# Diagonal 32x32 products and a small masked tile in the chunkwise recurrence

## The chip, the cores and the metric

The kernel runs on one core of one Trainium2 chip, in one launch. The metric is the device time of that core in microseconds (us). The engines are TensorE (PE, with its weight loads shown apart as PEld), VectorE (DVE), ScalarE (ACT), GpSimd (POOL) and SyncE (SP, which issues DMAs).

## The reference

The network has two layers over 1024 tokens of 1024 channels. The first mixes tokens with a gated linear recurrence (HGRN2), the second with a causal convolution; each is followed by a squared-ReLU MLP with 4096 hidden channels. The change touches the recurrence of the first layer alone:

```python
def chunkwise_gated_recurrence(q, k, v, b):      # chunks of C = 32, 8 heads, dk = dv = 128
    def step(S, inp):
        qc, kc, vc, bc = inp                     # bc: cumulative sum of log f inside the chunk
        diff = bc[..., :, None, :] - bc[..., None, :, :]
        decay = jnp.where(causal, jnp.exp(jnp.where(causal, diff, 0.0)), 0.0)
        scores = jnp.einsum('bhtd,bhsd,bhtsd->bhts', qc, kc, decay)
        o = (jnp.einsum('bhts,bhsv->bhtv', scores, vc)
             + jnp.einsum('bhtd,bhdv->bhtv', qc * jnp.exp(bc), S))
        b_last = bc[..., -1:, :]
        S = (jnp.exp(b_last)[..., 0, :, None] * S
             + jnp.einsum('bhsd,bhsv->bhdv', kc * jnp.exp(b_last - bc), vc))
        return S, o
    ...
```

`q` is the silu of one projection, `f` the forget gate, `k = 1 - f`. The weight of a pair (s, t), s not after t, is the product of q at t, k at s, and all gates between them, summed over the 128 channels.

## The kernel before

**The stage.** All engines' orders are written out by hand (`manual_schedule`). One stage of the program makes the projections q, forget and output gate of all eight heads from x, in products of 128x512 on PE (`pair_product`, line 815; tiles `xf` and `fs`, in 12 matmuls to a product). A product is four slots of three matmuls; after each slot, `slot` (line 842) advances a tick counter and, at a set pace, the recurrences that are under way (`recs`, `active`, `step`, line 827). So the matmuls of a recurrence stand between those of the projections in PE's queue. At most two heads are under way, and the second starts when the first has done LAG = 9 steps. A job given to `later(n, job)` (line 353) is recorded n ticks on; that is how work for DVE and ACT is set behind the matmuls that it reads. Beside the recurrence, DVE and ACT split the weights of the projections into two parts (`make_form`, lines 543 to 574: a cast on ACT at line 571 and a subtraction on DVE, tile `fs`) and take the products out of PSUM (`evacuate`, line 768: the copy `t<-ps` on ACT at line 781 or an addition on DVE). Three PSUM banks serve the projection's products; a product's copy on ACT has to be done before a later product accumulates in the same bank, which is the next but one or later.

**One head's recurrence** (`recurrence(h)`, line 591) works on all 1024 tokens of the head at once, in chunks of P = 128 tokens, 8 chunks to a head (`2 * NTB`). Q and K hold channels on partitions and tokens along the free axis. The weights of a chunk, tile `A` (name `at`: partition s, chunk, t), are built level by level. At each level n the gates of half a block are multiplied into Q or K (`scale(n)`), and products of K and Q then give the weights of pairs whose distance that level covers:

- `levels(K, Q)` after scales 1, 2 and 4 gives pairs in one block of 16 but in different blocks of 8; `levels(kd[:, 1], kd[:, 0])` gives pairs in one block of 8; a second `levels(K, Q)`, after `scale(8)`, gives pairs in one block of 32 but in different blocks of 16. Each call is 8 matmuls of 128x128, one to a chunk, into `level_ps` (PSUM banks 3 and 4), all columns of it.
- After each, `put(i)` copies the wanted entries into `A` by `copy_predicated` with the i-th mask, on DVE, over 8 chunks x 128 columns = 1024 elements of each partition.
- Two loops (n = 32, 64; lines 653 to 659) add the pairs farther apart: 16 matmuls of 32x32 after `scale(16)` and 8 of 64x64 after `scale(32)`, written into `level_ps` at their place right of the diagonal, at partitions 0 and 64 for n = 32 and 0 for n = 64. The third mask takes in everything right of the blocks of 16, so `put(2)`, after `scale(64)`, lays these out as well.

PE is fed step by step; `scale(8)` and `put(1)` are recorded a tick after the first `levels`, `put(0)` a tick after the second, `scale(16)` a tick after the third, and `put(2)` a tick after the loop of 64. Since all three `levels` calls write the same part of `level_ps`, the second waits for `put(1)` and the third for `put(0)`.

Then K is transposed (`kt`, copied out by ACT at line 668), the state is carried from chunk to chunk (`outer`, `chain` on DVE, tile `state`), and `attend` multiplies `A` and the state with values and queries. ACT squares and scales the result (lines 679 and 685), it is transposed, and stored.

`A` is set to zero once, by POOL (line 940). The masks are three tiles of 128x128, loaded once by SP (line 939). Both lie in a room of tiles laid out from line 929.

Of the kernel before, what the change touches and what calls it, by code (L numbers as in the profile page):

```python
# [10 lines left out]
I32 = mybir.dt.int32  # L11
# [4 lines left out]
P = 128  # L16
# [5 lines left out]
NTB = HT // P  # L22
# [215 lines left out]
def body(ctx, tc, d, out):  # L238
    nc = tc.nc
# [53 lines left out]
    vector = Clocked(nc.vector, bg.dve, vector_cost)  # L293
    tensor = Clocked(nc.tensor, bg.pe, tensor_cost)
# [49 lines left out]
    wide_t, rows = (HT,), (NTB, P)  # L344
# [8 lines left out]
    def later(n, job):  # L353
        if n:
            waiting.append((ticks[0] + n, job))
        else:
            job()
# [99 lines left out]
    for k in range(4):  # L457
        c = slice((k % 2) * HT, (k % 2 + 1) * HT)
# [117 lines left out]
    level_ps, out_ps = (banks[:, k : k + 2].rearrange("p k (a b) -> p (k a) b", b=P) for k in (3, 5))  # L576
# [3 lines left out]
    def mul(o, a, b):  # L580
        vector.tensor_tensor(out=o, in0=a, in1=b, op=ALU.mult)

    def cutout(t, at, dims):
        return bass.AP(tensor=t.tensor, offset=t.offset + at, ap=[t.ap[0], *dims])

    def load_values(i, at=None):
        h, half = divmod(i, 2)
        vts[i] = vs() if at is None else at
        nc.sync.dma_start(out=vts[i], in_=vd[h // 4][half][:, :, h % 4 * P : (h % 4 + 1) * P])

    def recurrence(h):
        B = qk[h]
        Q, K = B[:, 0], B[:, 1]
        n2 = 2 * HT
        F, T = p1("f"), p1("T")
        totals = {1: F}
        at = 0
# [4 lines left out]
        def total(n):  # L602
            t = totals[n].rearrange("p (b s) -> p s b", s=2)
            mul(totals[2 * n], t[:, 0], t[:, 1])

        def scale(n):
            nb = n2 // (2 * n)
            o = cutout(Q, n, [[n2 - n, 2], [2 * n, nb], [1, n]])
            mul(o, o, cutout(totals[n], 0, [[1, 2], [2, nb], [0, n]]))

        def levels(a, b):
            for s in range(0, n2, P):
                tensor.matmul(level_ps[:, s // P, :], a[:, s : s + P], b[:, s : s + P], start=True, stop=True)

        def put(i):
            vector.copy_predicated(A, mask[:, i : i + 1, :].to_broadcast([P, 2 * NTB, P]).bitcast(I32), level_ps)

        vector.tensor_scalar(out=F, in0=K, scalar1=GATE_EPS, scalar2=None, op0=ALU.max)
        mul(Q, Q, F)
# [8 lines left out]
        rt, kd = p1("rt"), p1("kd")  # L628
# [7 lines left out]
        yield  # L636
        total(8)
        yield
        levels(K, Q)
        total(16)  # L640
        later(1, lambda: (scale(8), put(1)))
        yield
        levels(kd[:, 1], kd[:, 0])
        total(32)
        later(1, lambda: put(0))
        yield
        if h == H - 1:
            load_values(2 * h, F[:, :HT].rearrange("p (a b) -> p a b", a=NTB))
        levels(K, Q)
        total(64)  # L650
        later(1, lambda: scale(16))
        yield
        for n in (32, 64):
            for s in range(0, n2, 2 * n):
                c, r = divmod(s, P)
                tensor.matmul(level_ps[r : r + n, c, r + n : r + 2 * n], K[:, s : s + n], Q[:, s + n : s + 2 * n], start=True, stop=True)
            if n == 32:
                later(1, lambda: scale(32))
                yield
        dec = p1("dec")  # L660
        later(1, lambda: (scale(64), put(2), vector.tensor_copy(out=dec, in_=totals[P])))
        yield
        yield
        nk = 2 * NTB - 1
# [46 lines left out]
        def values(c):  # L711
            return vts[2 * h + c // NTB][:, c % NTB]
# [14 lines left out]
        def attend(cs):  # L727
            for c in cs:
                tensor.matmul(out_ps[:, c, :], A[:, c, :], values(c), start=True, stop=c == 0)
                if c:  # L730
# [96 lines left out]
    def step():  # L827
        if recs and (not active or len(active) == 1 and active[0][2] >= LAG):
            active.append([recs[0], recurrence(recs.pop(0)), 0])
        if not active:  # L830
            return False
        if not (len(active) == 1 and active[0][0] == H - 1 and active[0][2] >= LAG):
            alone[0] = not alone[0]
            if alone[0]:
                return True
        for one in list(active):
            one[2] += 1
            if next(one[1], one) is one:
                active.remove(one)
        return True  # L840
# [82 lines left out]
    for _ in range(5):  # L923
# [5 lines left out]
    p1 = Room(  # L929
        ((144, 152), (164, 172), (136, 144), (172, KBYTES)),  # L930
        {
            "qk": ((2, 2 * HT), 3), "kd": ((2, 2 * HT), 1), "at": (chunks, 1), "f": (two_t, 1), "T": (two_t, 1), "kt": (chunks, 1), "t": (wide_t, 4),
            "sq": (wide_t, 2), "u": (wide_t, 2), "mask": ((3, P), 1), "rt": ((2 * P,), 1), "state": ((P,), 8), "dec": ((2 * NTB,), 2),
        },
    )
    vs = ring((124, 126), rows, "v")
    mask = p1("mask")
    A = p1("at")
    nc.sync.dma_start(out=mask, in_=d["mask"])
    nc.gpsimd.memset(A, 0.0)  # L940
    for i in range(2):
        load_values(i)

# [52 lines left out]
    def gain(kb, name, layer):  # L996
        return vec(kb, f"{name}_g", layer), vec(kb + 4, f"{name}_b", layer)
# [75 lines left out]
    g, b = gain(192, "ln_mix", 0)  # L1073
# [257 lines left out]
    g, b = gain(184, "ln_ffn", 0)  # L1331
# [237 lines left out]
    g, b = gain(120, "ln_ffn", 1)  # L1569
# [22 lines left out]
def _layout(inputs):  # L1592
    import numpy as np

    i = {k: np.asarray(v) for k, v in inputs.items()}
    c = np.ascontiguousarray
    x = i["x"][0]
    r = {"x": c(x), "xT": c(x.reshape(2, HT, KB, P).transpose(0, 3, 2, 1))}
    w = i["a_w_in"][0]

    def cols(m, n):
        return m.reshape(KB, P, n, P).transpose(2, 1, 0, 3)

    def wide(m):
        return m.reshape(4, 2, P, 2, HT).transpose(3, 0, 2, 1, 4)

    q, f, g = [cols(w[:, k * D : (k + 1) * D], H).reshape(H, P, 2, HT).transpose(0, 2, 1, 3) for k in (0, 1, 3)]
    r["wp"] = c(np.stack([np.concatenate([q[j], f[j]] if kind == "q" else [g[2 * j], g[2 * j + 1]]) for kind, j in PAIRS]))
    r["wv"] = c(wide(w[:, 2 * D : 3 * D])).reshape(4, 2, P, 1024)
    r["wout"] = c(wide(i["a_w_out"][0])).reshape(2, 4, P, 1024)  # L1610
    r["wpw2"] = c(wide(i["b_w_pw2"][0])).reshape(2, 4, P, 1024)
    p = i["b_w_pw1"][0]
    r["wpw1"] = c(np.stack([cols(p[:, :D], KB), cols(p[:, D:], KB)], 1)).reshape(KB, 2, P, 1024)
    r["w1"] = c(cols(i["ffn_w1"][1], 32)).reshape(32, P, 1024)

    w1 = i["ffn_w1"][:1].reshape(1, 2, 4, P, NFC, 2, 2, P)
    r["w1q"] = c(w1.transpose(0, 4, 6, 1, 3, 5, 2, 7)).reshape(1, NFC, 4, P, 1024)
    w2 = i["ffn_w2"].reshape(2, NFC, 2, 2, P, 2, HT)
    r["w2"] = c(w2.transpose(0, 1, 5, 3, 4, 2, 6)).reshape(2, NFC, 4, P, 1024)

    def chan(v):
        return v.reshape(-1, P).T

    r["par"] = c(
        np.concatenate(
            [chan(i[n][0]) for n in ("a_norm_g", "a_lb_logits", "b_b_pw1", "b_b_dw", "b_ln_g", "b_ln_b")]
            + [i["b_w_dw"][0].reshape(TAPS, KB, P).transpose(2, 1, 0).reshape(P, KB * TAPS)],
            1,
        )
    )  # L1630
    s, t = np.arange(P)[:, None], np.arange(P)[None, :]
    m = np.zeros((P, 3, P), np.float32)
    m[:, 0] = (s // 8 == t // 8) & (s <= t)
    m[:, 1] = (s // 16 == t // 16) & (s // 8 < t // 8)
    m[:, 2] = s // 16 < t // 16
    r["mask"] = m
    for n in ("ln_mix_g", "ln_mix_b", "ln_ffn_g", "ln_ffn_b"):
        r[n] = c(i[n])
    r["b_pw2"] = c(i["b_b_pw2"])
    return r  # L1640
# [16 lines left out]
```

## Time and profile before

| What | us |
|---|---|
| median of 3 runs | 2118.72 (2116.82 to 2122.96) |
| the profiled execution's own time | 2120.82 |
| its span, first to last instruction | 2119.0 |
| stage of projections and recurrence, from the span's start | 88 to 450 |

Busy times in the span: PE 2086.5, PEld 1731.7, DVE 1447.1, ACT 1037.4, POOL 390.0. Busy time counts a moment once, however many instructions overlap in it. PE's fp32 matmuls of the recurrence each leave two records in the trace, so 8 matmuls show as x16. A row of the timeline gives the start, the time until the last of its instructions ended, and how many there are; since matmuls overlap, what a row costs PE is read from its start to the next row's start. In brackets stands how long the engine had been idle and what ended that. A row by form gives busy time, mean duration of one in ns, and idle time ahead of the group with its releasers.

### The profile page before, as it was taken

To read this page: it belongs to the slowest core of one execution; us is meant where nothing else is said; L and a number is where in the kernel's file an instruction comes from. 1 tells how busy PE (TensorE), PEld (TensorE's weight loads), DVE (VectorE), ACT (ScalarE), POOL (GpSimd) and SP (SyncE) were. 2 spreads that over 40 slices of the span, in tenths; PEclk is the share of its full clock that TensorE was granted. 3 is DMA by queue.
4 is the path that set the end of the run, shared out by engine and by line. 5 is a ranking of instruction groups with operands and counts; after the bars stand their busy time and mean duration, and the time that the engine had idled before them with its cause. 6 is when DMAs were issued, how large, how long until landed. Compare 5 with 4: busy or idle time off the path is not lost.

```text
span 2119.0 us, 27037 instructions
## 1 busy us (share of the span) xinstructions
PE 2086.5 (98%) x10056; PEld 1731.7 (82%) x10056; DVE 1447.1 (68%) x1868; ACT 1037.4 (49%) x1593; POOL 390.0 (18%) x384
## 2 busy tenths in 40 slices
PE   8999999999999999999999999999999999999998
PEld 7888787888888888888888888888878888888887
DVE  8697788877775665665666997899436443654456
ACT  5445454541465555544444677378443443433333
POOL 0112212201000000000002897299001000000001
PEclk9999999999999999999999999999999999999999
DMA  4778889771589786989997654564694987855542
GB/s 182 235 176 212 234 226 243 191 257 70 170 256 316 261 280 226 365 327 336 350 335 285 265 193 184 210 256 150 190 334 159 353 308 288 327 204 190 196 161 100
DMA packets 173494, 508.62 MB, mean 240 GB/s; under 512 B 16433, under 2 KB 45361, under 8 KB 172337
## 3 DMA queue, kind: packets, MB, share of 16 engines
q1 hardware_dynamic: 157872, 448.16, 59.0%
q0 software_dynamic: 15488, 58.72, 12.1%
q8 instruction: 79, 1.29, 0.2%
q14 instruction: 55, 0.44, 0.1%
HBM read 377.32 MB, written 196.61 MB: 271 GB/s over the span
## 4 chain that ended last, share of the span: by engine, by line
PE 78%; DVE 9%; DMA 6%; POOL 3%; issue 2%; ACT 2%; SPq 0%; DVEq 0%; POOLq 0%; ACTq 0%
PE ps L173 78%; POOL cb L173 3%; DVE qk L173 2%; DMA wa<-ready 1%; DMA raw<-in_w_dram 1%; DVE t L173 1%; DMA y<-kept 1%; DVE fs L173 1%; DMA vr<-in_wv_dram 1%; DMA hf<-ht 1%; DMA raw<-in_w1q_dram 1%; DVE xf L173 1%; DVE at L173 0%; DMA dh<-hf 0%; DVE vr L173 0%
## 5 line engine op out<-in xcount | busy, mean ns | idle before, releaser
L173 PE MATMUL ps<-dw,dh 128*128 128x512 f32 x2688 | 611.3, 389 | 0.0
L173 PEld LDWEIGHTS ps<-dw,dh 128*128 128x128 f32 x2688 | 504.1, 188 | 104.9 <-ACT dh L70 0.5
L173 PE MATMUL ps<-x1f,fw 128*128 128x512 f32 x1344 | 308.5, 390 | 1.1 <-DVE c L173 0.9
L173 PEld LDWEIGHTS ps<-x1f,fw 128*128 128x128 f32 x1344 | 251.2, 188 | 54.0 <-issue 1.3
L173 PE MATMUL ps<-xa,wa 128*128 128x512 f32 x1152 | 268.8, 392 | 0.0
L173 PE MATMUL ps<-xf,fs 128*128 128x512 f32 x1008 | 251.1, 400 | 1.7 <-ACT t L781 0.8
L173 PEld LDWEIGHTS ps<-xa,wa 128*128 128x128 f32 x1152 | 214.2, 188 | 43.5
L173 POOL TENSOR_TENSOR cb<-cb,prod 128x512 f32<-128x512 f32 x176 | 234.6, 1342 | 17.5 <-ACT prod L1425 7.0
L173 PEld LDWEIGHTS ps<-xf,fs 128*128 128x128 f32 x1008 | 185.6, 190 | 40.2 <-DVE t L173 2.2
L173 DVE TENSOR_TENSOR dh<-dh 128x1024 fp32r<-128x1024 f32 x112 | 136.4, 1222 | 114.5 <-ACT dh L70 113.8
L173 DVE TENSOR_TENSOR dw<-dr,dw 128x1024 fp32r<-128x1024 f32 x112 | 136.6, 1222 | 105.6 <-ACT dw L70 105.0
L173 DVE SCALAR_TENSOR_TENSOR ps<-u,par,ps 128x512 f32<-128x512 f32 x288 | 198.6, 748 | 9.9 <-ACT ps L1437 8.5
L70 ACT CAST dh<-dh 128x1024 fp32r<-128x1024 f32 x112 | 117.0, 1050 | 146.5 <-DMA dh<-hf 146.0
L70 ACT CAST dw<-dr 128x1024 fp32r<-128x1024 f32 x112 | 117.4, 1053 | 135.9 <-PE ps L173 124.5
L173 PE MATMUL ps<-xc,wa 128*128 128x512 f32 x768 | 174.4, 389 | 0.0
L474 POOL TENSOR_TENSOR mv<-mv,nhalf 128x1 f32<-128x1 f32 x32 | 45.2, 1414 | 686.3 <-DVE mv L173 686.3
L173 PEld LDWEIGHTS ps<-xc,wa 128*128 128x128 f32 x768 | 144.1, 188 | 29.9
L1425 ACT ACTIVATE prod<-u,par 128x512 f32<-128x512 f32 x176 | 125.4, 722 | 54.3 <-POOL cb L173 53.7
L173 DVE TENSOR_TENSOR wa<-raw,wa 128x1024 fp32r<-128x1024 f32 x51 | 66.5, 1306 | 67.9 <-ACT wa L70 67.8
L70 ACT CAST wa<-raw 128x1024 fp32r<-128x1024 f32 x51 | 53.6, 1050 | 117.5 <-PE ps L173 109.6
L1288 POOL COPY next<-ss 128x1 f32<-128x1 f32 x37 | 17.3, 467 | 410.9 <-DVE spare L173 259.6
L173 PE MATMUL ps<-w,oT 128*128 128x512 f32 x384 | 89.2, 391 | 0.8 <-ACT oT L872 0.8
(198 smaller groups left out, 2685.4 us busy)
## 6 DMA issues: line engine op xcount, KB each, us to landing
wa<-ready SPq DMA_DIRECT2D x122, 512.0 KB, 4.2
dh<-hf SPq DMA_DIRECT2D x112, 512.0 KB, 5.2
sum_w<-in_w_dram POOLq DMA_DIRECT2D x40, 1024.0 KB, 10.8
ready<-spare SPq DMA_DIRECT2D x74, 512.0 KB, 4.9
dr<-sum_w SPq DMA_DIRECT2D x64, 512.0 KB, 4.5
raw<-in_w_dram SPq DMA_DIRECT2D x51, 512.0 KB, 4.4
dr<-in_w_dram SPq DMA_DIRECT2D x48, 512.0 KB, 5.1
raw<-in_w1q_dram SPq DMA_DIRECT2D x36, 512.0 KB, 4.6
```

The costliest lines, as they stand in the source:

```text
L70: self.nc.scalar.copy(out=slot[:, 0, c], in_=raw[:, c])
L173: return op(*args, **kw)
L474: nc.gpsimd.tensor_tensor(out=dst, in0=src, in1=nhalf[:, :n], op=ALU.pow)
L1288: nc.gpsimd.tensor_copy(out=raw[:, :1], in_=now)
L1425: nc.scalar.activation(tp, u[:, k : k + HT], AF.Copy, scale=tap(j, k))
```

## The change

The three `levels` calls now make only the 32x32 blocks on the diagonal: 32 matmuls of 32x32 to a call instead of 8 of 128x128, each written at the partitions of its block (0, 32, 64 or 96 in turn) and in a 32-column part of `level_ps` of its own (0, 1 or 2). `put(i)` masks 8 x 32 = 256 elements of each partition into a new tile `blocks`, and `put(2)` moves from behind `scale(64)` to behind `scale(16)`. ACT then writes `A`: `lay(r)` copies four block rows, 32 partitions x 8 x 32, from `blocks` to the diagonal of `A`; `far(r)` copies three parts, 32 partitions x 8 x 96, 64 and 32, from `level_ps` to `A`, right of the diagonal blocks. The two loops for n = 32 and 64 are unchanged. The masks shrink to 3 x 32 columns, and POOL sets `blocks` to zero once.

In the order of the built program, nothing else differs: each of PE's 24 rows of 8 matmuls of 128x128 is one of 32 of 32x32 at the same place, DVE has the same number of instructions with `put(2)` earlier, ACT has seven copies more in each head. SP and POOL keep their order, with one memset more on POOL.

```diff
-        def levels(a, b):
-            for s in range(0, n2, P):
-                tensor.matmul(level_ps[:, s // P, :], a[:, s : s + P], b[:, s : s + P], start=True, stop=True)
+        def levels(i, a, b):
+            for s in range(0, n2, 32):
+                c, r = divmod(s, P)
+                tensor.matmul(level_ps[r : r + 32, c, 32 * i : 32 * i + 32], a[:, s : s + 32], b[:, s : s + 32], start=True, stop=True)

         def put(i):
-            vector.copy_predicated(A, mask[:, i : i + 1, :].to_broadcast([P, 2 * NTB, P]).bitcast(I32), level_ps)
+            near = mask[:, i : i + 1, :].to_broadcast([P, 2 * NTB, 32]).bitcast(I32)
+            vector.copy_predicated(blocks, near, level_ps[:, :, 32 * i : 32 * i + 32])
+
+        def lay(r):
+            nc.scalar.copy(out=A[r : r + 32, :, r : r + 32], in_=blocks[r : r + 32])
+
+        def far(r):
+            nc.scalar.copy(out=A[r : r + 32, :, r + 32 :], in_=level_ps[r : r + 32, :, r + 32 :])
...
-        levels(K, Q)
+        levels(1, K, Q)
         total(16)
         later(1, lambda: (scale(8), put(1)))
         yield
-        levels(kd[:, 1], kd[:, 0])
+        levels(0, kd[:, 1], kd[:, 0])
         total(32)
         later(1, lambda: put(0))
         yield
...
-        levels(K, Q)
+        levels(2, K, Q)
         total(64)
-        later(1, lambda: scale(16))
+        later(1, lambda: (scale(16), put(2)))
         yield
...
             if n == 32:
                 later(1, lambda: scale(32))
+                later(2, lambda: [lay(r) for r in range(0, P, 32)])
                 yield
         dec = p1("dec")
-        later(1, lambda: (scale(64), put(2), vector.tensor_copy(out=dec, in_=totals[P])))
+        later(1, lambda: (scale(64), vector.tensor_copy(out=dec, in_=totals[P])))
+        later(2, lambda: [far(r) for r in range(0, P - 32, 32)])
...
-            ... "mask": ((3, P), 1), ...
+            ... "mask": ((3, 32), 1), "blocks": ((2 * NTB, 32), 1), ...
...
+    nc.gpsimd.memset(blocks, 0.0)
...
-    s, t = np.arange(P)[:, None], np.arange(P)[None, :]
-    m = np.zeros((P, 3, P), np.float32)
+    s, t = np.arange(P)[:, None] % 32, np.arange(32)[None, :]
+    m = np.zeros((P, 3, 32), np.float32)
```

More of the change, by code (lines that the diff above doesn't have):

```diff
@@ L932, in body @@
             "qk": ((2, 2 * HT), 3), "kd": ((2, 2 * HT), 1), "at": (chunks, 1), "f": (two_t, 1), "T": (two_t, 1), "kt": (chunks, 1), "t": (wide_t, 4),
-            "sq": (wide_t, 2), "u": (wide_t, 2), "mask": ((3, P), 1), "rt": ((2 * P,), 1), "state": ((P,), 8), "dec": ((2 * NTB,), 2),
+            "sq": (wide_t, 2), "u": (wide_t, 2), "mask": ((3, 32), 1), "blocks": ((2 * NTB, 32), 1), "rt": ((2 * P,), 1), "state": ((P,), 8), "dec": ((2 * NTB,), 2),
         },
@@ L937, in body @@
     mask = p1("mask")
-    A = p1("at")
+    A, blocks = p1("at"), p1("blocks")
     nc.sync.dma_start(out=mask, in_=d["mask"])
     nc.gpsimd.memset(A, 0.0)
+    nc.gpsimd.memset(blocks, 0.0)
     for i in range(2):
```

## The prediction

> **What bounds the kernel now.** I read the page's first part, then the table of three stretches, then the waits of PE in the stage that the change touches. First the page, with busy time and share of the span, and the chain that ended last:
>
> ```profile
> PE 2086.5 (98%) x10056; PEld 1731.7 (82%) x10056; DVE 1447.1 (68%) x1868; ACT 1037.4 (49%) x1593; POOL 390.0 (18%) x384
> PE 78%; DVE 9%; DMA 6%; POOL 3%; issue 2%; ACT 2%; SPq 0%; DVEq 0%; POOLq 0%; ACTq 0%
> ```
>
> PE is the bound: a microsecond off its queue is worth nearly a microsecond, unless it turns into a wait. The stretches (PE, PEld, DVE, ACT and POOL busy, then granted clock and DMA share) show whether that holds in the recurrence:
>
> ```profile
> 0.00:88.00 88.00, 81.84 (x347) 65.75 (x348) 66.57 (x94) 43.23 (x66) 4.51 (x12) 1.00 0.56 187
> 88.00:450.00 362.00, 348.03 (x2238) 295.01 (x2236) 297.45 (x442) 178.24 (x417) 71.42 (x89) 0.99 0.83 226
> 450.00:2119.00 1669.00, 1656.65 (x7474) 1370.95 (x7474) 1083.08 (x1333) 815.89 (x1110) 314.12 (x283) 1.00 0.70 246
> ```
>
> From 88 to 450 us PE is busy 348.0 of 362.0, and DVE 297.5 (82%), the highest load that it has anywhere for long; ACT has half its time free. The last stretch is PE from end to end, so what this stage gives or loses is passed on. PE's 14.0 us of idle time here, by whom it waited for (us, times, longest):
>
> ```profile
> PE ps L173 <- ACT kt L668: 4.7, 3, 4.0
> PE ps L173 <- DVE state L173: 4.0, 3, 2.6
> PE ps L173 <- DVE qk L173: 1.0, 2, 0.6
> PE ps L173 <- DVE T L173: 0.9, 1, 0.9
> PE ps L173 <- ACT t L781: 0.8, 1, 0.8
> PE ps L173 <- DVE at L173: 0.5, 1, 0.5
> ```
>
> **The products on PE.** PE's timeline in the first head, two rows of the fifth head, and a narrow look at the end of the small block:
>
> ```profile
> 129.11 2.99 PE L173 MATMUL ps<-xf,fs 128*128 128x512 f32 x12
> 131.94 1.95 PE L173 MATMUL ps<-qk 128*128 128x128 f32 x16
> 133.64 2.30 PE L173 MATMUL ps<-xf,fs 128*128 128x512 f32 x9
> 135.87 0.70 PE L173 MATMUL ps<-qk 128*32 128x32 f32 x32
> 136.37 0.20 PE L173 MATMUL ps<-qk 128*32 128x32 f32 x2
> 136.50 2.33 PE L173 MATMUL ps<-xf,fs 128*128 128x512 f32 x9
> 139.40 1.15 PE L173 MATMUL ps<-qk 128*64 128x64 f32 x16 [0.57 <-DVE qk L173]
> 298.17 2.98 PE L173 MATMUL ps<-xf,fs 128*128 128x512 f32 x12
> 301.08 0.70 PE L173 MATMUL ps<-qk 128*32 128x32 f32 x32
> ```
>
> A `levels` call of today takes from 131.94 to 133.64: 1.70 us for 8 matmuls (16 records). The loop for n = 32 already does what the change is made of: 16 matmuls of 32x32 (32 records), from 135.87 to 136.50, 0.63 us. The new call has twice as many, 64 records. If all of 0.63 doubles, it takes 1.26. If the way out is paid once (the last records start at 136.37, the next row 0.13 later), it is 63 steps of 0.50 / 31 = 0.016, and 0.13: 1.15. Going in costs too: 12 projection matmuls ahead of a 128-wide block take 131.94 - 129.11 = 2.83, ahead of a 32-wide one 301.08 - 298.17 = 2.91, so 0.08 more. A new call thus takes 1.23 to 1.34. I take 1.28, which saves 0.42; times 3 calls and 8 heads, **-10.1 us** (bounds -8.6 and -11.3).
>
> What is not seen: the loop of today writes at partitions 0 and 64 in turn, the new call at 0, 32, 64 and 96. The narrow look shows records two by two, so two column parts do overlap; more overlap with four is a rival below.
>
> **The masks on DVE.** Rows by form, mean ns of one:
>
> ```profile
> L173 DVE COPY_PREDICATED at<-mask,ps 128x1024 f32<-128x1024 int32 x24 | 32.5, 1354 | 6.2 <-PE ps L173 6.1
> L173 DVE TENSOR_TENSOR qk<-qk,T 128x1024 f32<-128x1024 f32 x48 | 58.7, 1223 | 34.8 <-PE ps L173 34.5
> L173 DVE TENSOR_TENSOR fs<-pr,fs 128x512 fp32r<-128x512 f32 x70 | 48.0, 685 | 20.0 <-ACT fs L571 19.8
> L173 DVE TENSOR_TENSOR T<-T 128x256 f32<-128x256 f32 x8 | 3.4, 427 | 0.0
> ```
>
> A masked copy of 256 elements isn't in the trace. An element costs (1223 - 685) / 512 = 1.05 ns, so 1354 less 768 of them is 0.55 us; the 256-wide product took 0.43; straight proportion would be 0.34. I take 0.50, so DVE is rid of 24 x 0.85 = 20.4 us. None of that counts by itself; it counts where PE waits for DVE.
>
> Two waits go outright. The second `levels` had to wait for `put(1)` (the 0.5 by `at`), the third for `put(0)` (the 0.9 by `T`, which stands right behind that mask in DVE's queue). The calls now write columns of their own, and Q is scaled ahead of `put(1)`: **-1.4 us**.
>
> Other waits are a DVE queue that is late from the third `levels` on. The third head shows it:
>
> ```profile
> 208.27 1.23 DVE L173 TENSOR_TENSOR qk<-qk,T 128x1024 f32<-128x1024 f32 x1 [1.69 <-PE ps L173]
> 213.08 1.22 DVE L173 TENSOR_TENSOR qk<-qk,T 128x1024 f32<-128x1024 f32 x1
> 214.49 1.15 PE L173 MATMUL ps<-qk 128*64 128x64 f32 x16
> 217.09 1.35 DVE L173 COPY_PREDICATED at<-mask,ps 128x1024 f32<-128x1024 int32 x1
> 233.05 0.49 PE L173 MATMUL ps<-state,qk 128*128 128x128 f32 x2 [2.62 <-DVE state L173]
> ```
>
> DVE works nearly without a pause from 208.27 to the `state` that PE awaits at 233.05. In that stretch one mask of 1.35 goes and one of 0.50 comes: PE gets its state 0.85 earlier. The same holds for the fifth head (`state`, the next longest) and the sixth (`kt`, 4.0, which stands in ACT's queue behind work that waits for DVE). Three times 0.85: **-2.6 us**. The rest of the 14.0 I leave as it is.
>
> **What the moved mask costs.** `put(2)` now stands ahead of `scale(32)` in DVE's queue, and the 64x64 products wait for `scale(32)`. In the third head that scale ends at 213.08 + 1.22 = 214.30, against a start at 214.49: 0.2 of slack for 0.5 of work. In the first head the 0.57 above becomes 1.07; in the fifth its wait (the other one of the two under `DVE qk`) grows by 0.5 as well. In the last head:
>
> ```profile
> 428.12 1.22 DVE L173 TENSOR_TENSOR qk<-qk,T 128x1024 f32<-128x1024 f32 x1
> 429.39 1.15 PE L173 MATMUL ps<-qk 128*64 128x64 f32 x16
> ```
>
> It ends at 429.34 with 0.05 of slack, so 0.45 is lost. Those of the third and fifth head lie in late stretches, where the 0.5 is counted already. Left are the first and the last: **+1.0 us**. The new wait of the 64x64 products for `put(2)` itself (they write its columns) ends before that, since it is queued ahead of `scale(32)`.
>
> **What ACT takes on.** Rows of its copies:
>
> ```profile
> L571 ACT CAST fs<-pr 128x512 fp32r<-128x512 f32 x70 | 42.9, 626 | 24.9 <-DVE pr L173 24.9
> L781 ACT COPY t<-ps 128x512 f32<-128x512 f32 x36 | 21.2, 588 | 14.9 <-PE ps L173 14.9
> L668 ACT COPY kt<-ps 128x896 f32<-128x896 f32 x8 | 7.2, 900 | 2.4 <-issue 2.0 <-PE ps L173 0.4
> L872 ACT CAST w<-raw 128x1024 fp32r<-128x1024 f32 x4 | 4.1, 1050 | 1.3 <-PE ps L173 1.3
> 141.49 0.59 ACT L781 COPY t<-ps 128x512 f32<-128x512 f32 x1 [0.88 <-PE ps L173]
> ```
>
> From PSUM an element costs (900 - 588) / 384 = 0.81 ns: copies of 768, 512 and 256 elements take 0.80, 0.59 and 0.38, together 1.76 for `far`. From SBUF (1050 - 626) / 512 = 0.83 ns: 0.41, times four 1.66 for `lay`. I suppose that 32 partitions cost what 128 do. That is 3.4 us a head, 27 in all; ACT goes from 178 to 205 of 362. `lay` waits for `put(2)`, but in the first head it stands behind an ACT instruction whose DVE source comes later than `put(2)`, so it adds no wait. `far` waits for the 64x64 products. Behind both stand the casts `fs`, made several products ahead, and the copies `t<-ps`, which PE needs when it comes back to that bank: one product (2.9 us) later, less 0.59 for the copy, so 2.3 us of cover. In the first head the copy of 141.49 would find ACT in `far` until about 139.40 + 1.15 + 0.5 + 1.8 = 142.8: 1.3 late, covered. I set **+1.0 us** for places where it isn't (bounds 0 and 27).
>
> `blocks` set to zero by POOL, and the smaller mask load, lie ahead of the stage, where POOL is busy 4.5 of 88 us: nothing.
>
> **Sum.** -10.1 - 1.4 - 2.6 + 1.0 + 1.0 = **-12.1 us**. The profiled execution took 2120.82 (2119.0 between its first and last instruction), so it would be 2108.7; against the median of 2118.72 it is **2106.6**. About 0.3%, 6.4 us, can be told from no change here, so this is twice that.
>
> **The rivals.** *More overlap with four column parts.* If 64 records take the 0.63 of 32, a call saves 1.70 - 0.71 = 0.99, 23.8 us in all: with the other terms 2093. The Trainium skill (TensorEngine Tiling (Array Packing), Key Properties) has different tiles of the array load and multiply independently, which speaks for it. Against it stands the pairing at 135.87: each matmul's two records use one column part, so the second waits for the first and holds up the queue, however many parts there are. Chance 0.08.
>
> *PE's idle time goes entirely*, because a shorter DVE queue removes more than its own 0.85: the six rows quoted sum to 11.9, with the products 22: 2097. The late `kt` and `state` would need 2 to 3 us more than I find. Chance 0.06.
>
> *The change doesn't shorten the products.* If a record cannot start less than some 25 ns after the last, 64 of them take 1.60, with the ways in and out 1.81: 0.11 more than now, 24 times +2.6; with the other terms +0.6, 2119.3. The Trainium skill (TensorE: Matmul & The Clock Gate, the section on 56 against 53.3 ns) puts the least distance of two starts at about 25 ns; the trace's 0.63 / 32 = 20 ns already goes below it. A front end that falls behind in a row of 64 would do the same. Chance 0.17.
>
> *ACT becomes the bound (slower).* If `lay` and `far` come ahead of the copies `t<-ps` in each head, and the PE stands for all of it, 27.3 comes on top of -10.1 - 4.0 + 1.0: +14, 2133. It decides when ACT reaches such a copy more than 2.3 us after its product's end. For it: the 0.8 that PE already waits for `t`, and the strict order of ACT. Against it: half of ACT's time is free, and it mostly waits for PE or DVE in front of these copies. Chance 0.11; 0.09 of it slower by over 0.3%, 0.02 in part only.
>
> **The numbers.** My forecast has 0.58, its own range 2101 to 2112. Faster by over 0.3%: 0.58 + 0.08 + 0.06 = 0.72; within 0.3%: 0.17 + 0.02 = 0.19; slower 0.09. The range 2095 to 2120 takes in the forecast, most of the case without idle time, and the case of no shorter products.
>
> **What would show it.** In the profile after: each call from its start to the next row 1.15 to 1.26 with 64 records (0.6: the overlap rival; 1.6 and more: the floor); masked copies of 0.4 to 0.55; no PE wait by `at` or a mask ahead of the second and third call; waits of the 64x64 products for `DVE qk` of 1 us in the first head and some 0.4 in the last; `state` waits shorter by 0.85; ACT about 205 in the stage and PE waits by `ACT t` below 2 us. I am wrong if these waits pass 5 us, or if small records cost more than 20 ns in long rows.

## The result, and the profile after

| | before | after |
|---|---|---|
| median, us | 2118.31 (2116.82 to 2122.96) | 2094.40 (2090.57 to 2095.18) |
| profiled execution, us | 2120.82 | 2094.47 |
| its span / PE busy / rest, us | 2119.0 / 2086.5 / 32.5 | 2092.7 / 2063.7 / 29.0 |

The ratio is 0.988, with a 95% interval of 0.986 to 0.9899: 24 us faster. The forecast was 2106.6 with a range of 2095 to 2120, so the direction was right, the size half of what came, and the time lies just below the range. Two executions of the kernel with ACT's copies twice (below) took 3469 and 8633 us and are left out of its ratio. The last row of the table says where the gain came from: of the 26.3 us between the two spans, 22.8 are PE's busy time and 3.5 its idle time. The page of the kernel after, busy times and chain:

```profile
PE 2063.7 (99%) x11208; PEld 1705.2 (81%) x11208; DVE 1427.4 (68%) x1868; ACT 1064.4 (51%) x1649; POOL 392.3 (19%) x385
PE 83%; DVE 7%; DMA 3%; POOL 3%; ACT 2%; issue 1%; SPq 0%; DVEq 0%; POOLq 0%; ACTq 0%
```

DVE lost 19.7 us and ACT gained 27.0, as worked out ahead (20.4 and 27); PE has 1152 records more and is busy for less time. PE's timeline of the first head after:

```profile
123.14 0.76 PE L173 MATMUL ps<-qk 128*32 128x32 f32 x64
123.84 2.34 PE L173 MATMUL ps<-xf,fs 128*128 128x512 f32 x9
126.41 0.76 PE L173 MATMUL ps<-kd 128*32 128x32 f32 x64 [0.23 <-DVE blocks L173]
127.10 3.02 PE L173 MATMUL ps<-xf,fs 128*128 128x512 f32 x12
130.05 0.76 PE L173 MATMUL ps<-qk 128*32 128x32 f32 x64
130.74 2.35 PE L173 MATMUL ps<-xf,fs 128*128 128x512 f32 x9
136.67 1.15 PE L173 MATMUL ps<-qk 128*64 128x64 f32 x16 [0.66 <-DVE qk L173]
```

From start to the next row's start, a call takes 0.70, 0.69, 0.69 us for 64 records, where 1.15 to 1.26 had been forecast: hardly more than the 0.63 that 32 such records take in the loop for n = 32. Times 24, 1.70 - 0.69 = 1.01 is 24.2 us. Going in costs about what was thought: the 12 projection matmuls from 127.10 to 130.05 take 2.95, against 2.83 ahead of a wide block, so 0.12 for the 0.08 of the forecast; 24 times that would bring the 24.2 down to 21.3, near the 22.8 of PE's busy time. And PE's waits in the stage, after:

```profile
PE ps L173 <- ACT kt L678: 3.5, 3, 2.8
PE ps L173 <- DVE state L173: 3.3, 2, 2.5
PE ps L173 <- DVE qk L173: 1.2, 2, 0.7
PE ps L173 <- issue: 0.5, 1, 0.5
PE ps L173 <- DVE blocks L173: 0.5, 2, 0.2
PE ps L173 <- DVE t L173: 0.4, 1, 0.4
```

`kt` and `state` fell from 8.7 to 6.8 together, the wait for `t` on ACT is gone, `DVE qk` grew by 0.2. Two places at which the prediction took 0.85 off, in the third and the sixth head:

```profile
223.16 0.49 PE L173 MATMUL ps<-state,qk 128*128 128x128 f32 x2 [2.50 <-DVE state L173]
339.19 1.29 PE L173 MATMUL ps<-v,kt 128*128 128x128 f32 x8 [2.80 <-ACT kt L678]
```

These waits were 2.62 and 3.96. The new pieces, by form, mean ns of one:

```profile
L173 DVE COPY_PREDICATED blocks<-mask,ps 128x256 f32<-128x256 int32 x24 | 10.6, 443 | 5.5 <-PE ps L173 5.5
L621 ACT COPY at<-blocks 32x256 f32<-32x256 f32 x32 | 12.8, 400 | 0.3
L624 ACT COPY at<-ps 32x768 f32<-32x768 f32 x8 | 6.3, 789 | 2.0 <-PE ps L173 1.9
L624 ACT COPY at<-ps 32x512 f32<-32x512 f32 x8 | 4.6, 578 | 0.1
L624 ACT COPY at<-ps 32x256 f32<-32x256 f32 x8 | 2.9, 364 | 0.1
```

A small mask takes 0.44 (0.50 was taken), and copies of 32 partitions cost what the 128-partition rows gave.

### The profile page after: what moved, and what is told of

Its sections match the earlier page's. It is cut to its first block, busy times and chain, and to the rows that moved or that the text cites. A ratio compares the mean times of both kernels' runs of the same rounds, so it can differ in the third digit from the quotient of the medians.

```text
span 2092.7 us, 29395 instructions
## 1 busy us (share of the span) xinstructions
PE 2063.7 (99%) x11208; PEld 1705.2 (81%) x11208; DVE 1427.4 (68%) x1868; ACT 1064.4 (51%) x1649; POOL 392.3 (19%) x385
## 4 chain that ended last, share of the span: by engine, by line
PE 83%; DVE 7%; DMA 3%; POOL 3%; ACT 2%; issue 1%; SPq 0%; DVEq 0%; POOLq 0%; ACTq 0%
PE ps L173 83%; POOL cb L173 3%; DVE qk L173 1%; DMA raw<-in_w_dram 1%; DMA wa<-ready 1%; DMA vr<-in_wv_dram 1%; DVE t L173 1%; DVE fs L173 1%; DVE xf L173 0%; DVE vr L173 0%; DVE pr L173 0%; DVE wa L173 0%; DVE rt L173 0%; DVE xr L173 0%; DVE ps L173 0%
## 5 line engine op out<-in xcount | busy, mean ns | idle before, releaser
L173 PEld LDWEIGHTS ps<-x1f,fw 128*128 128x128 f32 x1344 | 251.4, 188 | 53.3 <-issue 1.4
```

The costliest lines, as they stand in the source:

```text
L173: return op(*args, **kw)
```

## The experiments

The question was first why 64 records take 0.69 us, and then how the gain divides between PE, DVE and ACT. A column part is here what a 32-wide product uses: the 32 PSUM partitions that it is written to. Theory A has the four column parts working beside each other, and the products as nearly the whole gain. Theory B gives half of it to DVE's shorter masks, theory C has a limit on the distance of starts and not on parts. In the runs on ACT the letters A, D and E stand for what their expectations say.

**The products alone** (e1_products_alone). On the kernel before:

```diff
-            for s in range(0, n2, P):
-                tensor.matmul(level_ps[:, s // P, :], a[:, s : s + P], b[:, s : s + P], start=True, stop=True)
+            for s in range(0, n2, 32):
+                c, r = divmod(s, P)
+                tensor.matmul(level_ps[r : r + 32, c, r : r + 32], a[:, s : s + 32], b[:, s : s + 32], start=True, stop=True)
```

> The kernel before with 32x32 products on the diagonal, written in place in level_ps; masks, their size and place, and all else as before. Theory A (four column parts of the array work beside each other, the products are nearly the whole gain): a call takes 0.69 us as in the changed kernel, less some 0.12 for going in and out of small blocks, 24 x 0.89 = 21 us less than before, about 2097. Theory B (the shorter masks on DVE bring half of it): 12 us less, about 2106.

Measured: 2099.94, ratio 0.9917 (0.9899 to 0.9935), 18.8 us less by the medians and 22.2 by the profiled executions. The page's first row of this kernel, and its second call in the first head:

```profile
PE 2064.0 (98%) x11208; PEld 1705.3 (81%) x11208; DVE 1447.5 (69%) x1868; ACT 1036.5 (49%) x1593; POOL 396.5 (19%) x384
125.93 0.76 PE L173 MATMUL ps<-kd 128*32 128x32 f32 x64 [1.11 <-DVE at L173]
```

PE's busy time is that of the changed kernel to 0.3 us, DVE's and ACT's are those of before. The idle rest of the span is 2096.8 - 2064.0 = 32.8, as before (32.5). So about four fifths of the gain are the products, and the other 4 to 5.5 us need the rest of the change. The faster PE now meets the wide mask earlier: the wait for `at`, 0.52 before at this place, is 1.11.

**One column part at a time** (e2_one_part), **and two** (e3_two_parts). On the kernel after, the order of a call's products alone:

```diff
-            for s in range(0, n2, 32):
+            for s in [c * P + r for r in range(0, P, 32) for c in range(2 * NTB)]:                      # e2
+            for s in [c * P + r + q for r in (0, 64) for c in range(2 * NTB) for q in (0, 32)]:         # e3
```

> The changed kernel with the 32 products of a call in another order: all eight at partitions 0, then all at 32, 64, 96. Same instructions, same data. Theory A (a part works one record off in about 0.031 us, parts beside each other): no overlap, a call takes 64 x 0.031 + 0.13 = 2.1 us, 1.4 more, 24 times 34: about 2129, slower than before. Theory C (a start every 9 ns is the limit, whatever the part): 0.69, about 2094.

> The changed kernel with the products of a call in pairs: partitions 0 and 32 in turn for all chunks, then 64 and 96 in turn, as the loop for n = 32 has them. Theory A: half the overlap, 1.15 us a call, 0.46 more, 24 times 11: about 2105, which is where the prediction's term for the products lay. Theory C: 0.69, about 2094.

Measured: 2119.46, ratio 1.0003 (0.9994 to 1.0013), and 2101.40, ratio 0.9921 (0.9906 to 0.9936). The first call of the first head with one part, then with two:

```profile
123.33 1.91 PE L173 MATMUL ps<-qk 128*32 128x32 f32 x64
125.17 2.33 PE L173 MATMUL ps<-xf,fs 128*128 128x512 f32 x9
```

```profile
121.67 1.11 PE L173 MATMUL ps<-qk 128*32 128x32 f32 x64
122.71 2.33 PE L173 MATMUL ps<-xf,fs 128*128 128x512 f32 x9
```

The same 64 records take 1.84, 1.04 and (as changed) 0.69 us. With 0.13 for the way out, that is 27, 14.4 and 8.9 ns from one start to the next. So the order alone makes the difference, and theory C falls. Cut to 20 ns, the timeline lists the records that started in about the last 0.2 us; with one part, two and four these are:

```profile
123.41 0.39 PE L173 MATMUL ps<-qk 128*32 128x32 f32 x7
121.75 0.39 PE L173 MATMUL ps<-qk 128*32 128x32 f32 x14
123.25 0.41 PE L173 MATMUL ps<-qk 128*32 128x32 f32 x25
```

Single records of the traces show the steps. With one part they start 31 or 32 ns apart, but for three places in a row, near the changes of part, with starts 5 to 7 ns after the last; these bring the mean down to 27. With two parts the steps are 7 and 25 in turn, with four 7, 7, 6 and 12 (first half of a row). So each part starts a record every 32 ns, and the parts share these 32 ns. The three orders also differ in which chunk comes next; the loop for n = 32, with other addresses and two parts in turn, has the steps 7 and 25 as well.

With one part at a time the whole gain is gone, although the masks are still the small ones. Theory A had expected more, 2129, from 31 ns for every record. e3 comes near to what the prediction had thought the change to be (1.15 to 1.26 a call, forecast 2106.6): 1.04 a call, 2101.4.

**DVE's time** (e4_masks_thrice). On the kernel after:

```diff
-            vector.copy_predicated(blocks, near, level_ps[:, :, 32 * i : 32 * i + 32])
+            for _ in range(3):
+                vector.copy_predicated(blocks, near, level_ps[:, :, 32 * i : 32 * i + 32])
```

> The changed kernel with each masked copy made three times over (same result): DVE spends 1.33 us on a level instead of 0.44, about as much as before. Theory A: DVE's relief is worth little, the waits go back to those of before and the 64x64 products wait 0.9 longer: +3 to +6, about 2098 to 2100. Theory B (half of the gain is DVE's): +12, about 2106.

Measured: 2104.82, ratio 0.9936 (0.9921 to 0.9951), 10.4 us more than the changed kernel for 24 x 2 x 0.443 = 21.3 us of DVE work. PE's waits:

```profile
PE ps L173 <- DVE qk L173: 4.2, 5, 1.5
PE ps L173 <- ACT kt L679: 4.1, 3, 3.4
PE ps L173 <- DVE state L173: 3.9, 3, 2.5
PE ps L173 <- DVE blocks L173: 3.4, 5, 1.3
```

PE's idle rest goes from 29.0 to 2101.9 - 2063.3 = 38.6. Of these 9.6 us, 3.0 are the 64x64 products that wait for the scale behind the thrice-made `put(2)`, and 2.9 are the mask itself (`blocks`), above all ahead of the second call and of the loop of 32. This is nearer to theory B's size than to A's: with a faster PE, half of what DVE has more is paid.

**ACT's copies twice** (e5_copies_twice) **and left out** (e6_no_copies). On the kernel after:

```diff
-                later(2, lambda: [lay(r) for r in range(0, P, 32)])
+                later(2, lambda: [lay(r) for _ in range(2) for r in range(0, P, 32)])      # e5; no such line in e6
...
-        later(2, lambda: [far(r) for r in range(0, P - 32, 32)])
+        later(2, lambda: [far(r) for _ in range(2) for r in range(0, P - 32, 32)])         # e5; no such line in e6
```

> The changed kernel with lay and far made twice over on ACT (same result), 26.6 us more of ACT work in the stage. Theory A (ACT's copies lie in its idle time, nothing waits for them): 0 to +1 us, about 2094 to 2095.5. Theory D (the prediction's fear: copies t<-ps come late behind them): PE waits by ACT t appear, +3 us or more.

> The changed kernel without lay and far: the weights of the chunks' inner part stay zero, so that part of the computation is left out. ACT has 26.6 us less to do. Theory A: the copies cost nothing, within 1 us of 2094.4. Theory D: they cost 1 us or more, which comes back here: 2093 or less, above all at the kt wait, whose copy stands behind them in ACT's queue.

Measured: 2116.89, ratio 0.9991 (0.9981 to 1.0), and 2091.06, ratio 0.987 (0.9856 to 0.9883). With the copies twice, PE's waits, and a piece of the first head:

```profile
PE ps L173 <- ACT kt L678: 11.1, 5, 4.5
PE ps L173 <- ACT t L791: 6.0, 3, 2.8
PE ps L173 <- DVE state L173: 3.5, 2, 2.5
PE ps L173 <- DVE t L173: 3.5, 4, 1.9
```

```profile
138.43 3.57 ACT L624 COPY at<-ps 32x768 f32<-32x768 f32 x6
...
142.03 0.59 ACT L791 COPY t<-ps 128x512 f32<-128x512 f32 x1
...
142.66 1.67 PE L173 MATMUL ps<-xf,fs 128*128 128x512 f32 x6 [1.98 <-ACT t L791]
```

This is the prediction's slower rival, seen at twice the load: `far` holds ACT's queue for 3.6 us, the copy of a product behind it comes late, and PE stands for 2.0 us. 26.6 us of ACT work cost 22. At the single load there is no wait for `t` on ACT at all. Left out (`A` then stays zero, so this part of the recurrence is not computed), they bring some 3 us; the waits of that kernel that changed most:

```profile
PE ps L173 <- ACT kt L676: 3.0, 2, 2.9
PE ps L173 <- DVE state L173: 2.6, 1, 2.6
```

`kt` has 0.5 less than after, `state` 0.7, and the 0.4 for `t` is gone: 1.6 us can be named. The idle rest of the span is 26.5, 2.5 less than after. So the first copies cost some 3 us by the medians and the second ones 22: ACT's free half had room for about one such load. The 3 us are at the edge of what can be told: single runs of this kernel took 2089.4 to 2093.2, those of the changed kernel 2090.6 to 2095.2.

**The last mask put later** (e7_mask_late), **with two copies of DVE given to ACT** (e8_mask_late_act). On the kernel after:

```diff
+        def at(i):
+            return slice(32, 64) if i == 0 else slice(0, 32)      # columns of level_ps, in levels and put
...
-        later(1, lambda: (scale(16), put(2)))
+        later(1, lambda: scale(16))
...
-                later(1, lambda: scale(32))
+                later(1, lambda: (scale(32), put(2)))
... e8 also:
-        later(1, lambda: (scale(64), vector.tensor_copy(out=dec, in_=totals[P])))
+        later(1, lambda: (scale(64), nc.scalar.copy(out=dec, in_=totals[P])))
...
-                    vector.tensor_copy(out=new, in_=state_ps[:, 0])
+                    nc.scalar.copy(out=new, in_=state_ps[:, 0])
```

> The changed kernel with put(2) behind scale(32) in DVE's queue, and the third call in columns 0 to 32 of level_ps, which the loop of 64 doesn't write, so that no matmul waits for this mask. If the moved mask costs what the prediction says (0.45 to 0.5 at the 64x64 products of the first, fifth and last head, less where the stretch is late anyway): the DVE qk waits of 1.2 us fall to about 0.2, the total by 0.5 to 1.2 us, about 2093.5. If the wait only moves on to state and kt: 2094.4.

> As the one with put(2) behind scale(32), and DVE's two plain copies of a head (dec, 0.2 us, and the first state, 0.28 us) given to ACT. Where DVE is late at state, 0.2 to 0.5 comes off each of three waits, about 1 us below that kernel: 2092.5. Against it: ACT's copy of the first state has to wait its turn in ACT's queue, and would then make state later, +1.

Measured: 2103.51, ratio 0.9933 (0.9921 to 0.9946), and 2102.75, ratio 0.9924 (0.9912 to 0.9937). Both miss: the first is 9 us slower than the changed kernel, not 1 faster, and the second gives none of it back beyond the noise. A wait of ACT, three of PE's and a piece of the first head of e7 point to the reason:

```profile
ACT at L624 <- DVE blocks L173: 15.3, 8, 2.3
PE ps L173 <- ACT kt L681: 7.1, 5, 4.7
PE ps L173 <- DVE t L173: 2.5, 4, 1.6
PE ps L173 <- ACT t L794: 2.4, 3, 1.1
```

```profile
136.01 0.43 DVE L173 COPY_PREDICATED blocks<-mask,ps 128x256 f32<-128x256 int32 x1
136.34 0.68 DVE L173 TENSOR_TENSOR t<-t,ps 128x512 f32<-128x512 f32 x1
136.50 1.15 PE L173 MATMUL ps<-qk 128*64 128x64 f32 x16 [0.74 <-DVE blocks L173]
136.53 1.65 ACT L624 COPY at<-blocks 32x256 f32<-32x256 f32 x4 [2.19 <-DVE blocks L173]
...
138.19 0.62 ACT L571 CAST fs<-pr 128x512 fp32r<-128x512 f32 x1
...
138.85 0.69 DVE L173 TENSOR_TENSOR fs<-pr,fs 128x512 fp32r<-128x512 f32 x1 [1.83 <-ACT fs L571]
```

`lay` now stands at the head of ACT's queue for 2.2 us until the mask is there, the cast `fs` behind it starts at 138.19, and DVE waits 1.83 for that cast. PE then waits longer for `kt` and `t`, 8.1 us more than in the changed kernel. This is read from the trace; `lay` put later with the mask was not tried. And the 64x64 products still wait for the mask, though they write columns 64 to 128 of `level_ps` and the mask reads 0 to 32: the built program orders the two all the same. With `lay` where it stands, having `put(2)` ahead of `scale(32)` is thus worth 9 us and not a cost.

**ACT's copies spread out** (e9_spread, e10_spread_late), with **the changed kernel again** (e11_again). On the kernel after:

```diff
-                later(2, lambda: [lay(r) for r in range(0, P, 32)])
+                for r in range(0, P, 32):                  # e10: behind far, later(4 + r // 32, ...)
+                    later(2 + r // 32, lambda r=r: lay(r))
...
-        later(2, lambda: [far(r) for r in range(0, P - 32, 32)])
+        for r in range(0, P - 32, 32):
+            later(2 + r // 32, lambda r=r: far(r))
```

> The changed kernel with the four lay copies recorded one tick after another (2 to 5 after the loop of 32) and the three far copies too (2 to 4 after the loop of 64), instead of all in one tick, so that casts and copies t<-ps come in between on ACT. Theory E (ACT's copies cost some 3 us by holding up kt, t and fs for up to 1.7 us at a time; this is what the kernel without them gained): half of it comes back, 1 to 2 us less, about 2093. Theory A (they cost nothing, and the 3 us of the kernel without them were its missing data or noise): the same, 2094.4.

> As the spread kernel, but lay only after far (ticks 4 to 7 after the loop of 64). Theory E: ACT is freer between the third call and the 64x64 products, but the copies now stand closer to kt: between 2092 and 2096, and in the last head attend may wait for them, up to 2 us. Theory A: 2094.4 and a wait in the last head at most.

> The changed kernel itself once more, as the measure for the two spread kernels on one chip: ratio to before 0.988, about 2094.

Measured: 2094.63, ratio 0.9886 (0.9869 to 0.9902); 2092.80, ratio 0.988 (0.9862 to 0.9898); and 2094.72, ratio 0.9886 (0.9868 to 0.9904). No difference can be told. Spreading the copies brings back nothing that shows, so either the 3 us of the copies are not their standing in one row, or the copies cost nearly nothing; these runs do not settle which. No version here is clearly faster than the changed kernel.

## Why the prediction was half the size

- **The bound was right.** PE's queue sets the time, and what the stage gives is passed on: of 26.3 us, 22.8 are PE's busy time.
- **The step that failed is the time of a call**, -10.1 us for all, where PE's busy time fell by 22.8. The prediction took 64 records as twice 32 and set the overlap of four parts aside with this sentence: "each matmul's two records use one column part, so the second waits for the first and holds up the queue, however many parts there are". The one-part and two-part orders show which half is false. Records in one part do follow each other at 32 ns, but they don't hold up the queue: with four parts in turn three other records start within that time, and the means are 27, 14.4 and 8.9 ns a record with one, two and four parts. The loop that it was drawn from uses two parts alone, so doubling its 0.63 us measured nothing of four. The rival that had it right (0.71 with the way in, 23.8 us in all, 2093) had a chance of 0.08. The Trainium skill (TensorEngine Tiling (Array Packing), Key Properties) says that different tiles can load weights and multiply in parallel; the traces agree, with four starts in 32 ns over four parts for one start in one part.
- **No floor at 25 ns.** That rival would have needed 1.60 us for 64 starts; 0.69 was measured. By the figure of the Trainium skill (TensorE: Matmul & The Clock Gate, the section on 56 against 53.3 ns), no two starts come closer than about 25 ns; records of the trace start 9 ns apart on average, some of them 6 or 7, so the trace and not the figure decides.
- **The masks on DVE** were right in length (0.44 for 0.50) and too small in worth. -3.0 net was forecast for the waits that go, shrink or grow. The whole change differs from its products alone by 5.5 us by the medians (3.8 of idle time by the profiles), and ACT's copies cost nothing to some 3 of their own, so DVE's relief, with the waits that go, brought some 4 to 9 us; that last number is a sum of two experiments and not itself measured. The thrice-made masks point the same way, with 10.4 us.
- **The late `state` and `kt`** were to lose 0.85 at three places, -2.6. They lost 0.12 (third head), 0.32 (fifth, 1.16 to 0.84) and 1.16 (sixth), 1.6 in all. A likely reason, not tested: PE's queue got shorter by some 3 us a head as well, so PE comes earlier and waits for what DVE has gained. The terms beside the products sum to -2.0, against 3.5 us of idle time that went; with a relief that was too small and, perhaps, a price for ACT that was too small, that nearness is partly luck.
- **Two waits were to go outright.** One did (0.9 ahead of the third call). The second call still waits for `put(1)`, 0.23 in the first head, since the program orders them although the columns differ; it is shorter as the mask is, and 1.19 with the mask made thrice.
- **The moved mask** was forecast at +1.0; the waits of the 64x64 products grew from 1.0 to 1.2. The forecast missed what the place is good for: `lay` would otherwise hold up ACT.
- **ACT** was forecast at +1.0 with bounds of 0 and 27: some 3 by the medians, not clear of the spread of single runs. The cover of 2.3 us held at the single load (no wait for `t` on ACT), and failed at the double one.

## What to carry to other kernels

Where matmuls of 32 columns stand in a row, write them so that neighbours go to different 32-partition parts of PSUM: here the same products took 1.84, 1.04 or 0.69 us by their order alone. A rate that is read off an existing loop holds for that loop's pattern; ask what in it (two parts of four) set the rate before doubling it. An engine that is half idle may have room for work only once: here 26.6 us of copies on ACT cost at most some 3, the next 26.6 cost 22, and `lay` waiting at the head of ACT's queue went with 9 us more.

## What the runs showed that was not expected

- Small matmuls in four column parts start 8.9 ns apart on average, with one part 27 ns: each part starts one in 32 ns, and the parts do so beside each other.
- In the second head, the row of 32 records of the loop for n = 32 is broken after 14 of them by a pause in which PE waited for nothing that the profile shows. It stands at the same place in the order with two parts (0.35 us) and with the copies left out (1.09). In the changed kernel:

```profile
164.45 0.44 PE L173 MATMUL ps<-qk 128*32 128x32 f32 x14
165.37 0.50 PE L173 MATMUL ps<-qk 128*32 128x32 f32 x18 [0.48 <-issue]
```

It costs 0.35 to 1.14 us in the eight kernels that have it; e1, e2, e4 and e7 do not. The traces point to a cause that was not tested. The page's row of the queue that loads instructions (packets, MB, share), before and after:

```profile
q8 instruction: 79, 1.29, 0.2%
q8 instruction: 88, 1.44, 0.3%
```

The change adds instructions to PE above all, so the nine packets more are most likely PE's. In each of the eight, PE goes on 1.25 to 1.5 us after the end of such a packet (here 165.37 after 164.09), and so it does after a second pause of e5 (203.13 after 201.84). PE would then have stood for want of instructions.
